# Operands of the dense products at staggered byte offsets in a hybrid decoder trunk

## The chip, the cores and the metric

One core of one Trainium2 chip runs the whole kernel. The metric is the device time of one execution in microseconds (us). Times of single products are given in nanoseconds (ns). TensorE's clock has two levels, 1.2 and 2.4 GHz; the profile gives the granted clock as a share of the higher one.

## What is computed

Two pre-RMSNorm residual layers over 512 tokens of width 1024, and a last RMSNorm. Layer 0 mixes tokens with 8 stick-breaking and 8 sparse-attention heads, layer 1 with 16 forgetting-attention heads, and each layer ends with a gated MLP whose one branch runs through a causal convolution of width 3:

```python
def conv_glu_ffn(h, w_in, conv_w, conv_b, w_out):          # w_in 1024 x 5632, w_out 2816 x 1024
    a, b = jnp.split(h @ w_in, 2, axis=-1)
    a = conv_general_dilated(a, taps, padding=[(2, 0)], ...) + conv_b
    return (jax.nn.silu(a) * b) @ w_out

for layer in range(DEPTH):
    h = rmsnorm(x, attn_norm[layer])
    x = x + (even_mixer if layer % 2 == 0 else odd_mixer)(h, ...)   # h @ w_in, attention, o @ w_out
    x = x + conv_glu_ffn(rmsnorm(x, ffn_norm[layer]), ...)
return rmsnorm(x, final_norm)
```

All of it is float32. What the change touches are the dense products: `h @ w_in` and `o @ w_out` of both mixers, and the two products of each MLP.

## The kernel before

Activations lie transposed, channels on the 128 partitions and 512 tokens along them. The normed input is held in 8 chunks of 128 channels, and each chunk twice, split into a high part `XH[k]` and the rest `XL[k]` (`xh`, `xl` in the profile), both in the reduced format fp32r. A weight block is split in the same way: `weights` loads it as `wraw`, ScalarE casts it to the high part `whi` (L193), VectorE subtracts to get `wlo` (L194). A dense product is then three products on TensorE for each chunk, accumulated in one PSUM bank (`unit`):

```python
for k in range(NK):
    mm(ps, h[:, k], XH[k], k == 0, False)        # whi[k] loaded as weights, xh[k] moves
    mm(ps, l[:, k], XH[k], False, False)         # wlo[k] loaded, xh[k] moves
    mm(ps, h[:, k], XL[k], False, k == NK - 1)   # whi[k] loaded, xl[k] moves
```

`mm(out, l, r, ...)` (L115) is one weight load of 128 columns (`l`) and one product in which 512 columns of `r` move through the array. A unit is 24 such products. `proj` does the same for the output products, with the 11 chunks `gh`, `gl` of half an MLP's inner activation, or the attention's `oh`, `ol` (in layer 0 for the NSA heads `o4` and `o6`), in the place of `xh`, `xl`. `vgroup` turns the operands round: slices of `XH[k]` are loaded as weights and 256 to 272 columns of `whi` or `wlo` move. `finish` is the last two columns of blocks of the second MLP, in pieces of 320 and 192 columns.

The program runs in stages: layer 0's input products, its attention with dense units laid between the heads' work (`Fill` hands them out), its output product, the first MLP, layer 1 in the same order, the second MLP. In an MLP, `fl` holds 22 units of the input product for each half (11 pairs of `a` and `b`, `wfi`), then 8 of `proj`. `use_a` and `use_b` scale what a unit gives by `rstd`, convolve, apply SiLU and write `gh` (ScalarE, L795) and `gl` (VectorE, L796). All tiles come from pools that place them one behind another in each partition, so the size of a tile decides where the next one begins.

Below, **place** is the first byte of an operand in its partition, as the built program has it. Before, with c the chunk:

| operand | first place | next chunk | place modulo 256 |
|---|---|---|---|
| `xh` / `xl` | 26656 / 43040 | +2048 | 32 |
| `whi` (two buffers), `wlo` (two) | 89120, 93472; 97824, 102176 | +512 | 32 |
| `gh` / `gl` (14 buffers each) | 127008 / 155680 | +2048 | 32 |
| layer 0 `o4` / `o6` | 127008 / 172448 | +2048 | 32 / 160 |
| layer 1 `oh4` to `oh6`, `ol4` to `ol6` / `oh7`, `ol7` | 203424, 217760 / 223968, 226016 | +2048 | 160 / 224 |

While one product runs, the weights of the next one are loaded. The **distance** of a product is the place of its own moving operand less the place of the weights that the next product takes, modulo 256. Counted over the built program: 4153 fp32r products of 512 columns are followed by another fp32r product; 3847 of them have distance 0, and the other 306 belong to `oh`, `ol` and `o6`.

Of the kernel before, what the change touches and what calls it, by code (L numbers as in the profile page):

```python
# [10 lines left out]
F32R = mybir.dt.float32r  # L11
BF = mybir.dt.bfloat16
# [5 lines left out]
P = 128  # L18
SEQ = 512
D = 1024  # L20
NK = D // P
# [83 lines left out]
def trunk(ctx, tc, A):  # L105
# [3 lines left out]
    cp = EP(tc.tile_pool(name="cp", bufs=1))  # L109
    xp = EP(tc.tile_pool(name="xp", bufs=1))  # L110
    wp = EP(tc.tile_pool(name="wp", bufs=2))
    pp = EP(tc.tile_pool(name="pp", bufs=2, space=PSUM))

    def mm(out, l, r, st, sp_):
        pe.matmul(out, l, r, start=st, stop=sp_)  # L115
# [7 lines left out]
    def table(last=None):  # L123

        if last is None:
            return act.preload_act_table_set("natural_log_exp_and_others").ins
        with tc.issue_after(last):
            return act.preload_act_table_set("natural_log_exp_and_others").ins
# [18 lines left out]

        return xp.tile(shape, dt, tag=f"x{n}", name=name)

    XH = [xp.tile([P, SEQ], F32R, name=f"xh{c}") for c in range(NK)]  # L150
    XL = [xp.tile([P, SEQ], F32R, name=f"xl{c}") for c in range(NK)]
    ng = cp.tile([P, 5, NK], F32, name="ng")
    rstd = cp.tile([P, SEQ], F32, name="rstd")
    rtok = cp.tile([P, NB], F32, name="rtok")
# [12 lines left out]

    def warm():

        z = cp.tile([P, SEQ], BF, name="zero")  # L170
        pool.memset(z, 0.0)
        ps = pp.tile([P, SEQ], F32, tag="t", bufs=1, name="t")
        for n in range(12):
            mm(ps, z[:, 0:P], z, n == 0, n == 11)


    def weights(src, shape, alloc=None, pieces=1):

        w = wp.tile(shape, F32, tag="wraw", bufs=2, name="wraw")
        if pieces > 1:  # L180
            h = wp.tile(shape, F32R, tag="whi", bufs=2, name="whi")
            l = wp.tile(shape, F32R, tag="wlo", bufs=2, name="wlo")
            n = shape[1] // pieces
            for c in range(0, shape[1], n):
                sp.dma_start(w[:, c:c + n], src[:, c:c + n])
            return h, l, w
        sp.dma_start(w, src)
        if alloc is not None:
            h, l = alloc(shape)
        else:  # L190
            h = wp.tile(shape, F32R, tag="whi", bufs=2, name="whi")
            l = wp.tile(shape, F32R, tag="wlo", bufs=2, name="wlo")
        act.copy(h, w)  # L193
        dve.tensor_sub(l, w, h.bitcast(F32))  # L194
        return h, l

    def unit(src, use, ps=None, hl=None):

        h, l = weights(src, [P, NK, P]) if hl is None else hl
        yield  # L200
        ps = pp.tile([P, SEQ], F32, tag="mm", bufs=2, name="mm") if ps is None else ps()
        for k in range(NK):
            mm(ps, h[:, k], XH[k], k == 0, False)
            mm(ps, l[:, k], XH[k], False, False)
            mm(ps, h[:, k], XL[k], False, k == NK - 1)
            if k == NK - 1:
                use(ps)
            yield

    def vgroup(srcs, n, use, allocs=(None, None)):  # L210

        ws = [weights(s, [P, NK // 2, n], a) for s, a in zip(srcs, allocs)]
        yield
        for tb in range(NB):
            t = slice(tb * P, tb * P + P)
            ps = pp.tile([P, SEQ], F32, tag="mm", bufs=2, name="mm")
            for k in range(NK):
                h, l = ws[k // 4]
                o = ps[:, 0:n]
                mm(o, XH[k][:, t], h[:, k % 4], k == 0, False)  # L220
                mm(o, XH[k][:, t], l[:, k % 4], False, False)
                mm(o, XL[k][:, t], h[:, k % 4], False, k == NK - 1)
                if k == NK - 1:
                    use(tb, ps)
                if k % 2 == 1:
                    yield
# [14 lines left out]
    def feed(c, layer):  # L241

        scale_x(c, layer)
        squares(c)

    def scale_x(c, layer):
        g = ng[:, layer, c:c + 1]
        act.activation(XH[c], X[c], AF.Copy, scale=g)  # L248
        dve.scalar_tensor_tensor(XL[c], X[c], g, XH[c].bitcast(F32), op0=ALU.mult, op1=ALU.subtract)  # L249

# [80 lines left out]
    def norm_stats(tok):  # L331
        st = s_banks()
        ps, ps2 = st[:, 0], st[:, 1]
        mm(ps, ones, ACC[0], True, True)
        inv_sqrt(rstd, ps, SEQ)
        if tok:
            for tb in range(NB):
                mm(ps2[:, tb:tb + 1], ACC[0][:, tb * P:tb * P + P], ones[:, 0:1], True, True)
            inv_sqrt(rtok, ps2[:, :NB], NB)
# [133 lines left out]
    def proj(m, srcs, oh, ol, use=None, ready=None):  # L473

        n = len(oh)
        ws = [(weights(src, [P, kn, P]), kn) for src, kn in srcs]
        yield
        while ready is not None and not ready():
            yield "wait"
        ps = pp.tile([P, SEQ], F32, tag="mm", bufs=2, name="mm")  # L480
        k = 0
        for (h, l), kn in ws:
            for kk in range(kn):
                mm(ps, h[:, kk], oh[k], k == 0, False)
                mm(ps, l[:, kk], oh[k], False, False)
                mm(ps, h[:, kk], ol[k], False, k == n - 1)
                k += 1
                if k == n:
                    dve.tensor_add(X[m], X[m], ps)  # L489
                    if use is not None:  # L490
                        use(m)
                yield


    def layer0():
        with ExitStack() as es:
# [85 lines left out]
            load_x(True)  # L582
            table()
            warm()
            for c in range(NK):
                if c % 2 == 0:
# [181 lines left out]
    def ffn(layer, nl, final):  # L768
        with ExitStack() as es:
            fp = es.enter_context(tc.tile_pool(name=f"fp{layer}", bufs=2))  # L770
            fl = Fill()
            for half in range(2):
                GH, GL = [], []

                def pair(c):
                    cw = conv[:, layer, c]
                    box = []

                    def use_a(ps):
                        a = fp.tile([P, SEQ], F32, tag="a", bufs=2, name="a")  # L780
                        t = fp.tile([P, SEQ], F32, tag="tt", bufs=2, name="tt")
                        box.append(t)
                        dve.tensor_mul(a, ps, rstd)  # L783
                        act.activation(t, a, AF.Identity, bias=cw[:, 3:4], scale=cw[:, 2:3])
                        dve.scalar_tensor_tensor(t[:, 2:], a[:, :SEQ - 2], cw[:, 0:1], t[:, 2:], op0=ALU.mult, op1=ALU.add)
                        dve.scalar_tensor_tensor(t[:, 1:], a[:, :SEQ - 1], cw[:, 1:2], t[:, 1:], op0=ALU.mult, op1=ALU.add)  # L786
                        silu.append(act.activation(t, t, AF.Silu).ins)  # L787

                    def use_b(ps):
                        b = fp.tile([P, SEQ], F32, tag="b", bufs=2, name="b")  # L790
                        dve.tensor_mul(b, ps, rstd)  # L791
                        dve.tensor_mul(b, b, box[0])
                        gh = fp.tile([P, SEQ], F32R, tag="gh", bufs=14, name="gh")
                        gl = fp.tile([P, SEQ], F32R, tag="gl", bufs=14, name="gl")
                        act.copy(gh, b)  # L795
                        dve.tensor_sub(gl, b, gh.bitcast(F32))  # L796
                        GH.append(gh)
                        GL.append(gl)
                    return unit(A["wfi"][layer, 2 * c], use_a), unit(A["wfi"][layer, 2 * c + 1], use_b)

                for c in range(11 * half, 11 * half + 11):
                    fl.add(*pair(c))
                if not half:
                    fl.step(NK - 1)
                    norm_stats(False)
                fl.all()
                if half:
                    table(silu[-1])
                src = lambda m: [(A["wfo6"][layer, m, half], 6), (A["wfo5"][layer, m, half], 5)]
                use = (final if final else lambda m: feed(m, nl)) if half else None  # L810
                if half and final:
                    fl.add(*[proj(m, src(m), GH, GL, use) for m in range(NK - 2)])
                    fl.all()
                    finish(fp, src, GH, GL)
                    return
                fl.add(*[proj(m, src(m), GH, GL, use) for m in range(NK)])
                fl.all()

    ffn(0, 2, None)


# [120 lines left out]
    def last(m):  # L942

        squares(m)
        act.activation(X[m], X[m], AF.Copy, scale=ng[:, 4, m:m + 1])
    ffn(1, 4, last)


# [94 lines left out]
```

## Time and profile before

| what | value |
|---|---|
| median of 2 timed runs | 1290.58 us (1289.38 to 1291.78) |
| the profiled execution | 1291.93 us, span 1290.1 us from its first to its last instruction |
| TensorE busy | 1271.2 us, 99% of the span |
| VectorE / ScalarE / GpSimd busy | 693.7 / 555.7 / 147.9 us |
| granted clock | 0.997 on average |
| HBM | 119.28 MB read, 94 GB/s over the span with the writes |

The busy time of a product in this profile is modelled: products are pipelined, a row of 0.39 us overlaps the next one. What a product costs in a row of products is the step from its start to the next start, so the timelines below are read by their starts.

### The profile page before, as it was taken

Reading aid. Unit: us, or ns where it says so; the run is one execution under the profiler, and the core shown is the slowest. Engines: PE = TensorE matmul, PEld = TensorE weight load, DVE = VectorE, ACT = ScalarE, POOL = GpSimd, SP = SyncE. Lnnn points to the kernel's source line nnn. Section 1 sums busy time; section 2 is a strip of 40 time slices with the busy share of each in tenths; the row PEclk is TensorE's granted clock in tenths of the full one; section 3 lists DMA queues with packets and bytes.
Section 4 is the critical chain, followed back from the end, with each engine's and each line's share of the span. In section 5 each row is a group of like instructions: output and inputs, shape, how many; then the busy total and the mean of one; then the engine's idle time right before and its main releaser. Section 6 shows DMA issues by size and latency. Waiting matters only on the chain.

```text
span 1290.1 us, 16521 instructions
## 1 busy us (share of the span) xinstructions
PE 1271.2 (99%) x6338; PEld 1002.1 (78%) x6338; DVE 693.7 (54%) x1142; ACT 555.7 (43%) x948; POOL 147.9 (11%) x206
## 2 busy tenths in 40 slices
PE   8999999999999999999999999999999999999997
PEld 5876856567888888888888877866788888888886
DVE  7468665538655434565443443344755543556534
ACT  6556465645433223334342554444533322333442
POOL 0000042223000000000111433321200000000010
PEclk9999999999999999999999999999999999999999
DMA  6315201003333233232344453411333223333232
GB/s 224 95 59 147 87 21 42 19 26 123 98 99 94 78 106 107 92 98 89 94 127 141 145 151 92 120 51 51 122 98 98 88 90 100 108 94 94 88 99 90
DMA packets 50639, 124.00 MB, mean 96 GB/s; under 512 B 6320, under 2 KB 15792, under 8 KB 50560
## 3 DMA queue, kind: packets, MB, share of 16 engines
q1 hardware_dynamic: 49040, 121.35, 31.0%
q10 hardware_dynamic: 1520, 1.59, 0.4%
q8 instruction: 50, 0.82, 0.3%
q14 instruction: 29, 0.24, 0.1%
HBM read 119.28 MB, written 2.13 MB: 94 GB/s over the span
## 4 chain that ended last, share of the span: by engine, by line
PE 93%; DVE 3%; ACT 2%; issue 1%; DMA 1%; SPq 0%; DVEq 0%; ACTq 0%
PE mm L115 80%; PE s L115 6%; PE o L115 4%; PE t L425 3%; DVE e L462 1%; DVE wlo L194 0%; ACT whi L193 0%; DMA x<-x 0%; ACT xh L248 0%; DMA wraw<-wu 0%; DVE lt L457 0%; DVE acc L239 0%; ACT lt L454 0%; DVE e L463 0%; DVE e L401 0%
## 5 line engine op out<-in xcount | busy, mean ns | idle before, releaser
L115 PE MATMUL mm<-xh,whi 128*128 128x512 f32 x936 | 372.2, 398 | 0.9 <-ACT xh L248 0.6
L115 PE MATMUL mm<-xh,wlo 128*128 128x512 f32 x936 | 365.1, 390 | 1.6 <-DVE wlo L194 1.6
L115 PE MATMUL mm<-xl,whi 128*128 128x512 f32 x936 | 365.5, 391 | 0.1
L193 ACT CAST whi<-wraw 128x1024 fp32r<-128x1024 f32 (+2 forms) x219 | 200.0, 914 | 383.5 <-PE mm L115 362.7
L194 DVE TENSOR_TENSOR wlo<-wraw,whi 128x1024 fp32r<-128x1024 f32 (+2 forms) x219 | 236.4, 1079 | 137.4 <-ACT whi L193 134.7
L115 PEld LDWEIGHTS mm<-xh,whi 128*128 128x128 f32 x936 | 175.8, 188 | 44.8 <-issue 8.8
L115 PEld LDWEIGHTS mm<-xl,whi 128*128 128x128 f32 x936 | 175.8, 188 | 40.0 <-DVE xl L249 1.8
L115 PEld LDWEIGHTS mm<-xh,wlo 128*128 128x128 f32 x936 | 176.1, 188 | 37.0 <-DVE wlo L194 2.2
L115 PE MATMUL mm<-gh,whi 128*128 128x512 f32 (+2 forms) x352 | 135.0, 383 | 0.0
L115 PE MATMUL mm<-gl,whi 128*128 128x512 f32 (+2 forms) x352 | 134.8, 383 | 0.0
L115 PE MATMUL mm<-gh,wlo 128*128 128x512 f32 (+2 forms) x352 | 134.8, 383 | 0.0
L416 POOL TENSOR_SCALAR e<-e,dn 128x512 f32<-128x512 f32 (+3 forms) x128 | 78.1, 629 | 176.9 <-DVE dn L410 83.9
L403 ACT ACTIVATE e<-e,nm 128x512 f32<-128x512 f32 (+3 forms) x128 | 70.4, 551 | 50.2 <-DVE nm L401 50.2
L426 ACT COPY ph<-t 128x512 f32<-128x512 f32 x100 | 58.1, 581 | 69.6 <-PE t L425 69.4
L783 DVE TENSOR_TENSOR a<-mm,rstd 128x512 f32<-128x512 f32 x44 | 30.4, 691 | 92.1 <-PE mm L115 91.9
L237 POOL COPY acc<-sq 128x512 f32<-128x512 f32 x4 | 2.8, 706 | 651.4 <-ACT sq L234 651.4
L489 DVE TENSOR_TENSOR x<-x,mm 128x512 f32<-128x512 f32 x62 | 42.6, 686 | 64.2 <-PE mm L115 63.9
L115 PEld LDWEIGHTS mm<-gh,wlo 128*128 128x128 f32 x352 | 66.1, 188 | 13.0
L115 PEld LDWEIGHTS mm<-gl,whi 128*128 128x128 f32 x352 | 66.1, 188 | 12.8
L115 PEld LDWEIGHTS mm<-gh,whi 128*128 128x128 f32 x352 | 66.1, 188 | 12.8
L791 DVE TENSOR_TENSOR b<-mm,rstd 128x512 f32<-128x512 f32 x44 | 30.4, 692 | 72.4 <-PE mm L115 72.3
L787 ACT ACTIVATE tt<-tt 128x512 f32<-128x512 f32 x44 | 27.8, 632 | 86.8 <-DVE tt L786 86.8
(167 smaller groups left out, 1644.3 us busy)
## 6 DMA issues: line engine op xcount, KB each, us to landing
wraw<-wfi SPq DMA_DIRECT2D x88, 512.0 KB
wraw<-wu SPq DMA_DIRECT2D x31, 512.0 KB
wraw<-wfo SPq DMA_DIRECT2D x32, 384.0 KB
wraw<-wfo SPq DMA_DIRECT2D x32, 320.0 KB
wraw<-wo SPq DMA_DIRECT2D x32, 256.0 KB
cb<-cd SPq DMA_DIRECT2D x8, 512.0 KB
x<-x SPq DMA_DIRECT2D x14, 256.0 KB
wraw<-wv SPq DMA_DIRECT2D x6, 528.0 KB
```

The source lines that it names most:

```text
L115: pe.matmul(out, l, r, start=st, stop=sp_)
L193: act.copy(h, w)
L194: dve.tensor_sub(l, w, h.bitcast(F32))
L403: act.activation(ei, ei, AF.Exp, bias=nm, scale=-1.0, accum_out=dn)
L416: pool.tensor_scalar(ei, ei, self.dn[:, hd, i:i + 1], 1.0, op0=ALU.mult, op1=ALU.mult)
L425: pe.transpose(ps[:, o:o + P], self.e[:, hd, EOFF[i] + j * P:EOFF[i] + j * P + P], ident)
L426: act.copy(self.ph[:, 512 * n:512 * n + 512], ps)
L462: dve.tensor_tensor_scan(ei[:, ::-1], li[:, ::-1], li[:, ::-1], 0.0, op0=ALU.add, op1=ALU.bypass)
L489: dve.tensor_add(X[m], X[m], ps)
L783: dve.tensor_mul(a, ps, rstd)
L787: silu.append(act.activation(t, t, AF.Silu).ins)
L791: dve.tensor_mul(b, ps, rstd)
```

## The change

No instruction is added, taken away or moved: on each engine the two built programs list the same instructions in the same order, and they differ in where tiles lie in SBUF, and in one wait.

- `XH` and `XL` tiles get 8 more elements, so each chunk lies 2080 bytes behind the last instead of 2048. Chunk c begins at 25632 + 2080c (`xl`: 42272 + 2080c): modulo 256 that is 32 + 32c.
- `parts` allocates `whi` and `wlo` with 64 elements more than they need and puts the block `shift` elements in. In each half of an MLP the 22 units of the input product take the 22 pairs of `steps` (0 to 48 elements, 0 to 192 bytes, for `whi` and `wlo` apart); all other blocks take (0, 0). The buffers begin at 88608, 93216, 97824 and 102432, 32 modulo 256.
- `gh` and `gl` get 64 more elements, and chunk j of a half lies 4j bytes (`gh`) or 16j bytes (`gl`) into its place; the places themselves are 32 modulo 256 as before.
- `zero`, the operand of the warm-up products, moves from a pool of its own into the `sq` buffers. ScalarE's first square (L234) takes the same buffer and now waits for the warm-up products and the memset of `zero`.
- All tiles behind these move by 512 bytes, their places modulo 256 unchanged: `q`, `k`, `e`, `ph`, `oh`, `ol`, `o4`, `o6` and the rest.

By the built program, of the 3803 products of 512 columns in which `xh`, `xl`, `gh` or `gl` moves, 3801 had distance 0 before. Now 396 have it; 1857 have a distance from 96 to 224, and 1550 another one (4 to 92, or 228 to 252). The distance of a product in the input product changes with each chunk, that is after each third product.

```diff
-    XH = [xp.tile([P, SEQ], F32R, name=f"xh{c}") for c in range(NK)]
-    XL = [xp.tile([P, SEQ], F32R, name=f"xl{c}") for c in range(NK)]
+    XH = [xp.tile([P, SEQ + 8], F32R, name=f"xh{c}")[:, 0:SEQ] for c in range(NK)]
+    XL = [xp.tile([P, SEQ + 8], F32R, name=f"xl{c}")[:, 0:SEQ] for c in range(NK)]
...
-        z = cp.tile([P, SEQ], BF, name="zero")
+        z = wp.tile([P, SEQ], BF, tag="sq", bufs=2, name="zero")
...
+    SHIFT = [(0, 0)]
+
+    def parts(shape, shift):
+
+        n = shape[1] * shape[2]
+        out = []
+        for tag, o in zip(("whi", "wlo"), shift):
+            t = wp.tile([P, n + 64], F32R, tag=tag, bufs=2, name=tag)
+            out.append(t[:, o:o + n].rearrange("p (k m) -> p k m", m=shape[2]))
+        return out
...
+        shift = SHIFT.pop(0) if len(SHIFT) > 1 else SHIFT[0]
...
-            h = wp.tile(shape, F32R, tag="whi", bufs=2, name="whi")
-            l = wp.tile(shape, F32R, tag="wlo", bufs=2, name="wlo")
+            h, l = parts(shape, shift)
...
+                steps = ((0, 0), (0, 32), (32, 0), (0, 16), (16, 0), (0, 48), (48, 0), (0, 8), (8, 0), (0, 1), (1, 0),
+                         (0, 2), (2, 0), (0, 4), (4, 0), (4, 4), (8, 8), (16, 16), (24, 0), (0, 24), (40, 0), (0, 40))
+                SHIFT[:] = list(steps) + [(0, 0)]
...
-                        gh = fp.tile([P, SEQ], F32R, tag="gh", bufs=14, name="gh")
-                        gl = fp.tile([P, SEQ], F32R, tag="gl", bufs=14, name="gl")
+                        j = c % 11
+                        gh = fp.tile([P, SEQ + 64], F32R, tag="gh", bufs=14, name="gh")[:, j:j + SEQ]
+                        gl = fp.tile([P, SEQ + 64], F32R, tag="gl", bufs=14, name="gl")[:, 4 * j:4 * j + SEQ]
```

## Rows read from the trace of the kernel before

**Rows 1.** The page of the profile: busy time of each engine (its share of the span, its instructions), and the chain of work that ended last, by engine and by line.

```profile
PE 1271.2 (99%) x6338; PEld 1002.1 (78%) x6338; DVE 693.7 (54%) x1142; ACT 555.7 (43%) x948; POOL 147.9 (11%) x206
...
PE 93%; DVE 3%; ACT 2%; issue 1%; DMA 1%; SPq 0%; DVEq 0%; ACTq 0%
PE mm L115 80%; PE s L115 6%; PE o L115 4%; PE t L425 3%; DVE e L462 1%; DVE wlo L194 0%; ACT whi L193 0%; DMA x<-x 0%; ACT xh L248 0%; DMA wraw<-wu 0%; DVE lt L457 0%; DVE acc L239 0%; ACT lt L454 0%; DVE e L463 0%; DVE e L401 0%
```

**Rows 2.** Groups of TensorE's instructions over the whole span, shapes kept apart: line, engine, operation, result and operands (the moving one first, the one that is loaded as weights second), shape, count, then busy us, mean ns of one, and idle us of the engine just before them.

```profile
L115 PE MATMUL mm<-xh,whi 128*128 128x512 f32 x936 | 372.2, 398 | 0.9 <-ACT xh L248 0.6
L115 PE MATMUL mm<-xl,whi 128*128 128x512 f32 x936 | 365.5, 391 | 0.1
L115 PE MATMUL mm<-xh,wlo 128*128 128x512 f32 x936 | 365.1, 390 | 1.6 <-DVE wlo L194 1.6
L115 PE MATMUL mm<-gh,whi 128*128 128x512 f32 x330 | 128.4, 389 | 0.0
L115 PE MATMUL mm<-gl,whi 128*128 128x512 f32 x330 | 128.4, 389 | 0.0
L115 PE MATMUL mm<-gh,wlo 128*128 128x512 f32 x330 | 128.4, 389 | 0.0
```

**Rows 3.** TensorE's timeline over one unit of the first FFN's input product (24 products; the last row is the first product of the next unit): start in us, us of one, engine, line, operation, result and operands.

```profile
500.24 0.39 PE L115 MATMUL mm<-xh,whi 128*128 128x512 f32 x1
500.46 0.39 PE L115 MATMUL mm<-xh,wlo 128*128 128x512 f32 x1
500.69 0.39 PE L115 MATMUL mm<-xl,whi 128*128 128x512 f32 x1
...
505.68 0.39 PE L115 MATMUL mm<-xh,whi 128*128 128x512 f32 x1
```

**Rows 4.** Two stretches of 300 us, one in each FFN: start and end, length, TensorE's busy us and its products begun, granted clock as a share of full speed, DMA share and GB/s.

```profile
340.00:640.00 300.00, 300.00 (x1325) 1.00 0.31 96
960.00:1260.00 300.00, 300.00 (x1325) 1.00 0.32 96
```

**Rows 5.** TensorE's timeline at the first 32 products of `finish`, 320 columns wide: the first, and the last that is not merged with another kind.

```profile
1261.42 0.30 PE L115 MATMUL mm<-gh,fh 128*128 128x320 f32 x1
...
1266.11 0.31 PE L115 MATMUL mm<-gl,fh 128*128 128x320 f32 x1
```

**Rows 6.** TensorE's timeline over two units (24 products) of the output product of layer 1: the first, two in the middle, and the first of the next unit.

```profile
904.87 0.39 PE L115 MATMUL mm<-oh,whi 128*128 128x512 f32 x1
...
906.25 0.40 PE L115 MATMUL mm<-oh,whi 128*128 128x512 f32 x1
906.49 0.40 PE L115 MATMUL mm<-oh,wlo 128*128 128x512 f32 x1
...
910.44 0.39 PE L115 MATMUL mm<-oh,whi 128*128 128x512 f32 x1
```

**Rows 7.** TensorE's timeline where the output product of layer 0 ends (its last product starts at 308.29) and the first unit of the first FFN begins: its first, fourth and seventh product.

```profile
308.52 0.39 PE L115 MATMUL mm<-xh,whi 128*128 128x512 f32 x1
...
309.22 0.39 PE L115 MATMUL mm<-xh,whi 128*128 128x512 f32 x1
...
309.90 0.39 PE L115 MATMUL mm<-xh,whi 128*128 128x512 f32 x1
```

**Rows 8.** TensorE's timeline over 24 products of layer 0's second value group, where slices of `xh` and `xl` are loaded as weights and 264 columns of `vhi`, `vlo`, `whi` and `wlo` move: the first of three of the groups of three, the one behind them, and the first product of the next block of rows.

```profile
61.32 0.28 PE L115 MATMUL mm<-vhi,xh 128*128 128x264 f32 x1
...
61.68 0.28 PE L115 MATMUL mm<-vhi,xh 128*128 128x264 f32 x1
...
62.05 0.28 PE L115 MATMUL mm<-vhi,xh 128*128 128x264 f32 x1
...
62.40 0.28 PE L115 MATMUL mm<-vhi,xh 128*128 128x264 f32 x1
...
64.21 0.28 PE L115 MATMUL mm<-vhi,xh 128*128 128x264 f32 x1
```

**Rows 9.** The stretch of the first FFN: start and end, length, busy us and instructions of PE, PEld, DVE, ACT and POOL, granted clock, DMA share and GB/s.

```profile
308.50:667.00 358.50, 358.37 (x1579) 296.09 (x1578) 190.25 (x237) 128.44 (x162) 11.42 (x9) 1.00 0.32 98
```

**Rows 10.** Groups of VectorE's and ScalarE's instructions from 340 to 640 us that write the operands of the products: line, engine, operation, out<-in, shape, count, busy us, mean ns of one, idle us before them and what ended it.

```profile
L194 DVE TENSOR_TENSOR wlo<-wraw,whi 128x1024 fp32r<-128x1024 f32 (+2 forms) x63 | 68.4, 1086 | 43.2 <-ACT whi L193 42.1
L796 DVE TENSOR_TENSOR gl<-b,gh 128x512 fp32r<-128x512 f32 x20 | 13.7, 685 | 1.4 <-ACT gh L795 1.4
L193 ACT CAST whi<-wraw 128x1024 fp32r<-128x1024 f32 (+2 forms) x63 | 59.5, 944 | 145.2 <-PE mm L115 145.1
L795 ACT CAST gh<-b 128x512 fp32r<-128x512 f32 x20 | 12.5, 624 | 11.4 <-DVE b L792 11.4
```

**Rows 11.** The start: TensorE's warm-up products and ScalarE's first square, from the timelines of the two engines.

```profile
1.35 5.00 PE L115 MATMUL t<-zero 128*128 128x512 bf16 x12 [1.35 <-POOL zero L171]
...
12.26 0.61 ACT L234 ACTIVATE sq<-x 128x512 f32<-128x512 f32 x1
```

More of the change, by code (lines that the diff above doesn't have):

```diff
@@ L190, in weights @@
         else:
-            h = wp.tile(shape, F32R, tag="whi", bufs=2, name="whi")
-            l = wp.tile(shape, F32R, tag="wlo", bufs=2, name="wlo")
+            h, l = parts(shape, shift)
         act.copy(h, w)
```

## The prediction, made before the changed kernel was run

> **What bounds the kernel now.** I read the page first: TensorE is busy 99% of the span, 93% of the chain that ended last is on it, and 80% is the one line L115 with result `mm`, the dense products [rows 1]. Nothing else comes near, so what counts is what one dense product costs. The groups of TensorE's instructions say how many there are: 3 x 936 with `xh` or `xl` moving and 3 x 330 with `gh` or `gl`, 3798 in all, with idle time of 2.6 us in front of the first three groups together and none in front of the others [rows 2]. Their "mean ns" (389 to 398) can't be summed, since one product overlaps the next; the cost is the step from start to start.
>
> Step by step, then, on the timeline. A unit of 24 products in the MLP takes 505.68 - 500.24 = 5.44 us, 226.7 ns a product [rows 3]. Two stretches of 300 us hold 1325 products each, 226.4 ns with the ones at the edges counted whole, TensorE busy all the time at full granted clock, the level of 2.4 GHz [rows 4]. There is no jitter to win back there: nothing waits, and every step is the same. What of the 226.7 ns is columns? In `finish`, 320 columns take (1266.11 - 1261.42) / 32 = 146.6 ns [rows 5]. 192 columns less save 80.1 ns, 0.417 ns a column. So 512 columns are 213.5 ns, and **13.2 ns a product** don't depend on the width. These 13.2 ns are all that a change of places can act on: 3798 times, 50 us.
>
> **Do they depend on places?** The trace has three stretches in which distances are not 0.
> - Layer 1's output product, all distances 128 or 192: 24 products in 910.44 - 904.87 = 5.57 us, 232.1 ns each; single steps differ (906.25 to 906.49 is 240) [rows 6]. That is 5.4 ns a product above the MLP, with the same operations at the same width.
> - From such products into the MLP's, at distance 0: the first three steps take 309.22 - 308.52 = 0.70 us (233 ns each), the next three 0.68 (227) [rows 7]. So even at distance 0 the short step has to be reached, and it took three products.
> - The value group, 264 columns: 24 products in 64.21 - 61.32 = 2.89 us, 120.4 ns each. 264 columns are 110.1 ns by the price above, so 10.3 ns are left, less than 13.2, although the distances there run through all multiples of 32. Its groups of three differ: at distances 160, 32, 160 the three take 0.37 us (13.2 ns over the columns), at 192, 64, 192 0.35 us (6.6 ns over them) [rows 8].
>
> Places do matter, by a few ns a product, to both sides.
>
> **The change, part by part.** No instruction is added or moved, so its whole price is in the steps.
> 1. *Chunks 32 bytes apart, shifted weights, shifted `gh` and `gl`.* 3407 products leave distance 0 (1857 to distances from 96 to 224, 1550 to others), and nearly all the rest no longer stand in a row of equal distance. For a product of 512 columns at distance 128 or 192 there is a row: +5.4 ns. I take it for the 1857: 10.0 us. For the other 1550 no row has a product of this width at their distances. The bounds are +5.4 ns (as in rows 6, and as at the entry in rows 7) and -2.9 ns (10.3 against 13.2, as in rows 8). I take half of the loss, +2.7 ns, since rows 7 show that a new distance starts on a long step, and here a new one comes after each third product: 4.2 us. The 396 at distance 0 I leave. Sum **+14.2 us**. Bounds for all 3407: +5.4 ns is +18.4 us, -2.9 ns is -9.9 us, and the best group of three (-6.6 ns) would be -22.5 us.
> 2. *Writes of shifted operands.* ScalarE's casts and VectorE's subtractions write at odd multiples of 4 bytes. The trace has no such write. In the first MLP VectorE is busy 190 of 358 us and ScalarE 128 [rows 9]. If the groups that write `wlo` and `gl` cost twice as much, VectorE would have 82.1 us more in 300 [rows 10], a share of 53 + 27 = 80%; ScalarE 128 / 358 + 72 / 300, 60%. TensorE covers both, so 0. Without that cover it would be those microseconds.
> 3. *`zero` in the `sq` buffers.* The first square starts at 12.26, the warm-up products end at 6.35 [rows 11]. The new wait is over 5.9 us before it is reached; behind it nothing moves. 0.
> 4. *Value groups.* Their distances ran through all multiples of 32 and do so again in another order. 640 products by the difference of the groups of three (6.6 ns) would be 4 us either way; I take 0.
>
> Against the profiled execution: span 1290.1 + 14.2 = 1304.3, an execution of 1306.1. That execution (1291.93) lies 1.35 us above the median of the runs shown, so on that scale 1290.6 + 14.2 = 1304.8; I say 1304.
>
> **A rule that says otherwise.** The row: equal products take 226.7 or 232.1 ns, and the places of their operands are what differs [rows 3, 6]. The Trainium skill, "TensorE: Matmul & The Clock Gate", section "Step-by-step: what each phase is for", holds that TensorE reads the moving operand and the next weights through two independent ports, so that loading weights takes no read bandwidth from the running product. By that rule the sum of part 1 is 0; by the rows it is +14.2 us. The trace does not agree with the rule as far as it goes, and I follow the trace.
>
> **The rivals.**
> - *Nothing changes.* Layer 1's 232.1 ns might come from something else than distance: its operands lie elsewhere in SBUF, and other work runs beside it. Then the steps stay at 226.7 and the time is 1290.6. Against it: in rows 7 the same operands at the same place go from 233 to 227 ns within three products, so it is a state that two streams of reads fall into, and the groups of three in rows 8 differ by place alone. Some distances may also keep the short step, with a mean loss of 1 or 2 ns: 1294 to 1297.
> - *It gets faster.* If products of 512 columns at mixed distances behave as the value group does, each saves 2.9 ns: 1290.6 - 9.9 = 1280.7; with the price of the best three everywhere, 1268.1. It decides if the mean step in the MLP's input product falls below 226.7. For it: the value group is the one place where all distances occur. Against it: at a width of 512 no stretch shows less than 226.7, and distance 192, good in the value group, is in the slow rows of layer 1.
> - *It gets slower by more than 2%.* That needs 25.8 us, 7.6 ns on each of the 3407, a mean step of 234.3. Single steps of 240 exist [rows 6], a mean over a unit as high as that does not. It would take distances that no row shows, such as those of the weights and of `gh` that are no multiple of 16 bytes. With 240 in all of them: 1290.6 + 3407 x 13.3 = 1335.9.
> - *VectorE becomes the bound* in the MLP by slow shifted writes: worked out in part 2, needs more than a doubling. Very unlikely, and then a matter of some tens of us.
>
> **How the numbers follow.** A mean loss of 2.2 to 5.4 ns (1298 to 1309): 0.45, and its middle is the forecast. About nothing (1287 to 1298): 0.23. Faster, 1265 to 1287: 0.13. A loss beyond 5.4 ns but below 2% (1309 to 1316): 0.05. Slower by more than 2%: 0.10. Faster by more than 2% (below 1264.8; it needs the step at 219 ns, less than the best three): 0.04. The range from **1282 to 1316** leaves out about 0.08 below and 0.10 above, and holds both signs; the likeliest case alone is 1298 to 1309. About 2% is what a measurement of this kernel can tell from no change: faster 0.04, within it 0.86, slower 0.10.
>
> **What would show it.** In the changed profile the count of products is the same and so is the granted clock. Right: in the MLP a unit of 24 takes 5.50 to 5.57 us in place of 5.44, more where its chunks lie at distances from 96 to 224; two stretches of 300 us hold some 20 products fewer; layer 1's output product stays at 232 ns. Wrong in sign: units of 5.37 us, or groups of three at 220 ns. Wrong in place: gaps in front of `mm` with VectorE or ScalarE as the releaser, or a busy time of L194 and L193 that has grown by tens of us and shows up on the chain. The forecast fails if the short step holds at any distance, or if the distances without a row are much worse than 128 and 192.

## The result, and the profile after

| | before | after |
|---|---|---|
| median | 1290.58 us (1289.38 to 1291.78) | 1307.91 us (1307.88 to 1307.95) |
| span of the profiled execution | 1290.1 us | 1306.1 us |

The ratio is 1.0134, 95% interval 1.0091 to 1.0178: 17.3 us longer, and within 2%.

The page of the profile after: busy time of each engine, and the chain of work that ended last, by engine and by line.

```profile
PE 1288.0 (99%) x6338; PEld 1001.4 (77%) x6338; DVE 693.9 (53%) x1142; ACT 555.4 (43%) x948; POOL 146.7 (11%) x206
...
PE 95%; DVE 2%; ACT 2%; DMA 1%; issue 1%; SPq 0%; DVEq 0%
PE mm L115 81%; PE s L115 7%; PE o L115 4%; PE t L436 3%; DMA x<-x 0%; DVE e L473 0%; ACT xh L259 0%; ACT whi L204 0%; DMA wc<-wcv 0%; DVE acc L250 0%; DVE lt L468 0%; DVE wlo L205 0%; ACT lt L465 0%; DVE e L474 0%; DVE e L412 0%
```

TensorE is still the only bound, busy 99%; its busy time has grown by 16.8 us (1271.2 in [rows 1]), while VectorE and ScalarE are as before (693.7, 555.7). Groups of TensorE's instructions, shapes kept apart (busy us, mean ns of one, idle us in front):

```profile
L115 PE MATMUL mm<-xh,whi 128*128 128x512 f32 x936 | 376.1, 402 | 1.2 <-ACT xh L259 1.2
L115 PE MATMUL mm<-xl,whi 128*128 128x512 f32 x936 | 369.7, 395 | 0.1
L115 PE MATMUL mm<-xh,wlo 128*128 128x512 f32 x936 | 369.1, 394 | 1.4 <-DVE wlo L205 1.4
L115 PE MATMUL mm<-gh,whi 128*128 128x512 f32 x330 | 129.6, 393 | 0.0
```

Same counts as in [rows 2], no new idle time in front of them (2.7 us in all, 2.6 before), and each mean about 4 ns higher. So the time is in the products themselves. The two stretches of 300 us (TensorE's busy us, its products begun, granted clock, DMA share, GB/s):

```profile
340.00:640.00 300.00, 300.00 (x1294) 1.00 0.30 94
960.00:1260.00 300.00, 300.00 (x1295) 1.00 0.30 93
```

1294 and 1295 products instead of 1325 [rows 4], at the same full clock: 300 / 1294 = 231.8 ns each against 226.4, **5.4 ns more**. The MLPs hold 88 units of 24 and 990 output products, 3102 of 512 columns; 3102 x 5.4 = 16.8 us, which covers the 16.0 us of the span. By the first and last products on TensorE's timeline the first MLP goes from 360.35 to 368.67 us and the second, up to `finish`, from 350.23 to 358.24; what lies before the first MLP is 1.0 us shorter, layer 1's mixer 0.6 us longer, and the rest is the same. The 1.0 us says nothing of the change: that stretch took 308.5 us in this trace of the kernel before and 306.6 in the run with two pads (below), where nothing in it differs.

One unit of the first FFN on TensorE's timeline, with `whi` 64 and `wlo` 0 bytes into their places, all distances multiples of 32 (the first product, two in the middle, the first of the next unit):

```profile
514.65 0.40 PE L115 MATMUL mm<-xh,whi 128*128 128x512 f32 x1
...
516.76 0.40 PE L115 MATMUL mm<-xh,whi 128*128 128x512 f32 x1
517.00 0.39 PE L115 MATMUL mm<-xh,wlo 128*128 128x512 f32 x1
...
520.25 0.39 PE L115 MATMUL mm<-xh,whi 128*128 128x512 f32 x1
```

24 products take 5.60 us, 233 ns each; single steps go up to 0.24 us. In [rows 3] they took 5.44 and every step was alike. All the units of the MLP's input product that run without a gap lie between 5537 and 5606 ns, whatever their distances. Layer 1's output product, whose places the change leaves alone, over 24 products:

```profile
909.32 0.39 PE L115 MATMUL mm<-oh,whi 128*128 128x512 f32 x1
...
914.89 0.39 PE L115 MATMUL mm<-oh,whi 128*128 128x512 f32 x1
```

5.57 us, as in [rows 6]. Last, three groups that write the shifted operands, VectorE's and ScalarE's between 340 and 640 us (count, busy us, mean ns of one, idle us in front):

```profile
L205 DVE TENSOR_TENSOR wlo<-wraw,whi 128x1024 fp32r<-128x1024 f32 (+2 forms) x61 | 66.6, 1092 | 41.3 <-ACT whi L204 40.4
L204 ACT CAST whi<-wraw 128x1024 fp32r<-128x1024 f32 (+2 forms) x61 | 57.7, 945 | 147.2 <-PE mm L115 147.2
L811 ACT CAST gh<-b 128x512 fp32r<-128x512 f32 x20 | 12.4, 622 | 11.5 <-DVE b L807 11.5
```

1092, 945 and 622 ns against 1086, 944 and 624 in [rows 10]. The first two means mix block sizes, and few of their blocks stand at odd multiples of 4 bytes; `gh` does in every second chunk (`gl`, shifted by multiples of 16 bytes, never does). In the run below that shifts the weights by every multiple of 4 bytes, VectorE's `wlo` of 128x1024 takes 1223 ns against 1222 before, and ScalarE's `whi` 1050 against 1056. So writing to odd multiples of 4 bytes costs nothing that these rows show.

### The profile page after: what moved, and what is told of

The parts are those of the page before. It is cut to its first block, busy times and chain, and to the rows that moved or that the text cites. A ratio compares the mean times of both kernels' runs of the same rounds, so it can differ in the third digit from the quotient of the medians.

```text
span 1306.1 us, 16522 instructions
## 1 busy us (share of the span) xinstructions
PE 1288.0 (99%) x6338; PEld 1001.4 (77%) x6338; DVE 693.9 (53%) x1142; ACT 555.4 (43%) x948; POOL 146.7 (11%) x206
## 4 chain that ended last, share of the span: by engine, by line
PE 95%; DVE 2%; ACT 2%; DMA 1%; issue 1%; SPq 0%; DVEq 0%
PE mm L115 81%; PE s L115 7%; PE o L115 4%; PE t L436 3%; DMA x<-x 0%; DVE e L473 0%; ACT xh L259 0%; ACT whi L204 0%; DMA wc<-wcv 0%; DVE acc L250 0%; DVE lt L468 0%; DVE wlo L205 0%; ACT lt L465 0%; DVE e L474 0%; DVE e L412 0%
## 5 line engine op out<-in xcount | busy, mean ns | idle before, releaser
L115 PE MATMUL mm<-xh,whi 128*128 128x512 f32 x936 | 376.1, 402 | 1.2 <-ACT xh L259 1.2
L115 PE MATMUL mm<-xh,wlo 128*128 128x512 f32 x936 | 369.1, 394 | 1.4 <-DVE wlo L205 1.4
L115 PE MATMUL mm<-xl,whi 128*128 128x512 f32 x936 | 369.7, 395 | 0.1
L798 DVE TENSOR_TENSOR a<-mm,rstd 128x512 f32<-128x512 f32 x44 | 30.4, 691 | 97.7 <-PE mm L115 97.5
L806 DVE TENSOR_TENSOR b<-mm,rstd 128x512 f32<-128x512 f32 x44 | 30.4, 691 | 78.3 <-PE mm L115 78.3
```

## The experiments

The words of the theories: **D**, the loss is a matter of a product's own distance; **P**, of the place itself; **C**, of the distance changing from product to product. Later **S**: the short step needs distance 0 *and* each kind of operand at the same place (modulo 256) from product to product; **P2**: it needs the place 32.

### The parts of the change by themselves

Chunks 2080 bytes apart and nothing else shifted (`gh` and `gl` in their wide places, all 32 modulo 256):

```diff
-                SHIFT[:] = list(steps) + [(0, 0)]
-    gh = ...[:, j:j + SEQ]      gl = ...[:, 4 * j:4 * j + SEQ]
+    gh = ...[:, 0:SEQ]          gl = ...[:, 0:SEQ]
```

> One part of the change alone: chunks of xh and xl 2080 bytes apart; weight blocks unshifted; gh and gl in places of 2304 bytes but unshifted, so distance 0. Three theories. D (distance): the short step of 226.7 ns is reached only in a row of products at distance 0, all else runs near 232. P (place): the step depends on where an operand itself begins, not on the difference of two. C (change): a change of the distance from product to product costs, its value does not. All three expect the MLP's input product at about 232 ns a step (its unit of 24 at 5.56 us) and the MLP's output product, whose places are wider but whose distance is 0, back at 226.7 (33 products in 7.48 us). Time: about 12 us over before, 1301 to 1304. If the wider places of gh and gl mattered by themselves, the output product would not be back.

1304.63 us against 1289.73 for the kernel before in the same session, ratio 1.0114 (1.0099 to 1.0129): +14.9 us. 24 products of the output product, and a unit of the input product (TensorE's timeline: the first product of each, and the first behind it):

```profile
440.37 0.39 PE L115 MATMUL mm<-gh,whi 128*128 128x512 f32 x1
...
445.81 0.39 PE L115 MATMUL mm<-gh,whi 128*128 128x512 f32 x1
...
526.87 0.40 PE L115 MATMUL mm<-xh,whi 128*128 128x512 f32 x1
...
532.45 0.40 PE L115 MATMUL mm<-xh,whi 128*128 128x512 f32 x1
```

5.44 us where nothing is staggered, 5.58 where the chunks are. Every chunk then has its own distance, 0 among them; the unit repeats with one pattern of steps between 226 and 238 ns, and the three products at distance 0 take 231 ns on average, hardly less than the rest. 80 of the 88 units take 5580 ns to within 1 ns, whatever VectorE, ScalarE and the DMA do beside them, which speaks against a collision with their work. The 2304 bytes from one `gh` to the next do no harm: they are a multiple of 256.

Only `gh` and `gl` shifted, by 4j and 16j bytes:

```diff
-                SHIFT[:] = list(steps) + [(0, 0)]
-    XH = [xp.tile([P, SEQ + 8], ...)[:, 0:SEQ] ...]     (XL alike)
+    XH = [xp.tile([P, SEQ], ...)[:, 0:SEQ] ...]
```

> The other part alone: gh shifted by 4j bytes and gl by 16j, chunks of xh and xl 2048 apart and weight blocks unshifted. All three theories: input product at 226.7 ns a step, output product near 231.5; 990 products of about 4.9 ns more are 4.8 us, so about 1295.5. This and the chunks alone should add up to the change, with nothing left for the shifted weights, if a product that has lost the short step can lose it only once.

1295.57 us, ratio 1.0047 (1.003 to 1.0063): +5.8 us. The output product on TensorE's timeline:

```profile
440.10 0.39 PE L115 MATMUL mm<-gh,whi 128*128 128x512 f32 x1
...
445.66 0.39 PE L115 MATMUL mm<-gh,whi 128*128 128x512 f32 x1
```

5.56 us for 24, 231.7 ns each, while the input units are back at 5.44. 990 x 5 ns is 5.0 us, about what the time shows. The expectation that this and the chunks alone add up to the change can't be read from the times: 14.9 + 5.8 = 20.7 us against 17.3, with intervals of about 2 us on the parts and 6 on the whole. By the steps it holds: 88 units x 0.14 us is 12.3 us with the chunks, 5.0 us here, together 17.3, against 16.8 in the MLPs of the change. The shifts of the weights added nothing on top.

Only the weight parts' shifts in the units of the input product:

```diff
-    XH = [xp.tile([P, SEQ + 8], ...)[:, 0:SEQ] ...]     (XL alike)
-    ...[:, j:j + SEQ]      ...[:, 4 * j:4 * j + SEQ]
+    XH = [xp.tile([P, SEQ], ...)[:, 0:SEQ] ...]
+    ...[:, 0:SEQ]          ...[:, 0:SEQ]
```

> Only the third part of the change: the shifts of the weight parts, with chunks 2048 bytes apart and gh and gl unshifted. By counts 1150 products of the MLP's input product then stand at another distance than 0 and 880 of the same units still at 0. If each product pays by its own distance: 1150 x 5.6 ns = 6.4 us, units about 5518 ns, time 1297. Theory S (a product at another place also costs its neighbours the short step): all 84 shifted units at 5540 to 5600 ns, 11.7 us, time 1302. With the other two parts, 14.9 and 5.8 us by themselves, the sum is over the 17.3 us of the whole in both cases, since the chunks and the shifts act on the same products.

1299.15 us against 1289.41, ratio 1.0079 (1.0063 to 1.0095): +9.7 us, between the two expectations. First products of units on TensorE's timeline: with (`whi`, `wlo`) shifted by (0, 0), then by (0, 128) bytes, then the one behind; and of the unit with (16, 0), `whi` 16 bytes on and `wlo` in place, and the one behind it:

```profile
489.36 0.39 PE L115 MATMUL mm<-xh,whi 128*128 128x512 f32 x1
...
494.80 0.40 PE L115 MATMUL mm<-xh,whi 128*128 128x512 f32 x1
...
500.35 0.40 PE L115 MATMUL mm<-xh,whi 128*128 128x512 f32 x1
...
567.13 0.39 PE L115 MATMUL mm<-xh,whi 128*128 128x512 f32 x1
...
572.58 0.39 PE L115 MATMUL mm<-xh,whi 128*128 128x512 f32 x1
```

5.44 us, 5.55 us, and 5.45 us in the last. Most shifted units take 5527 to 5610 ns, as S expects; but with (16, 0) the steps are back at 227 ns from the third on, and the next unit, both parts 16 bytes on, goes on like that (5448 ns), and the one with (96, 0) takes 5513. So another place for the weights is not always a loss. The times of the three parts sum to 30.4 us where the whole is 17.3: chunks and weight shifts act on the same products, and a product loses its short step only once.

### Is it the distance?

Distance the same throughout a unit: chunks 2048 bytes apart, `gh` and `gl` unshifted, and both weight parts of a unit shifted by the same amount, 0 to 224 bytes in steps of 32:

```diff
+                steps = ((0, 0), (0, 0), (8, 8), (8, 8), (8, 8), (16, 16), ..., (56, 56), (56, 56))
```

> Chunks 2048 apart, gh and gl unshifted, and in each unit of the MLP's input product whi and wlo shifted by the same amount, two or three units in a row with 0, 32, 64, 96, 128, 160, 192 and 224 bytes. So the distance is the same for all 24 products of a unit and runs through all multiples of 32 from unit to unit. D expects 226.7 in the units at distance 0 and about 232 at all the others: 1280 products x 5.3 ns in each half of the kernel's two MLPs scaled to 1920 in all, 10 us, about 1301. C expects 226.7 everywhere but for three or so products behind each change: 1291 to 1292. P expects long steps wherever the weights are shifted, as D. A distance with a step under 226.7, which none of the three asks for, would be of use.

1301.56 us (one execution). Units at distance 0 and at distance 64 (weights shifted by 192 bytes) on TensorE's timeline, first product and first of the next:

```profile
490.62 0.39 PE L115 MATMUL mm<-xh,whi 128*128 128x512 f32 x1
...
496.06 0.39 PE L115 MATMUL mm<-xh,whi 128*128 128x512 f32 x1
...
585.40 0.39 PE L115 MATMUL mm<-xh,whi 128*128 128x512 f32 x1
...
590.89 0.39 PE L115 MATMUL mm<-xh,whi 128*128 128x512 f32 x1
```

5.44 and 5.49 us. All other distances settle between 5571 and 5626 ns: a distance that stays the same is not enough, so C falls. Each unit falls into a short pattern that repeats (232, 235, 232, 235 at a shift of 32 bytes; 226, 229, 232 at distance 64).

The opposite: distance 0 everywhere, with places that move on. `xh` and the weights' chunks are staggered together by 32 bytes a chunk (the weights' chunks 544 bytes apart), `xl` 32 bytes further on than `xh`, so that it too meets its next weights at distance 0:

```diff
+        m = shape[2] + (8 if shape[1:] == [NK, P] else 0)
+            out.append(t.rearrange("p (k m) -> p k m", m=m)[:, :, 0:shape[2]])
```

> Moving chunks and weight chunks staggered together: chunk c of xh 32c bytes on, chunk k of whi and wlo 32k bytes on (544 bytes from one to the next), xl 32 bytes further on than xh, so that each product finds its next weights at distance 0 although the places of both run through all multiples of 32 as in the change. gh and gl unshifted. D and C expect 226.7 ns a step everywhere, 1290 to 1292. P expects the input product as in the change, near 232, about 1302.

1303.42 us, ratio 1.0106 (1.0091 to 1.0121). A unit, on the timeline:

```profile
512.93 0.39 PE L115 MATMUL mm<-xh,whi 128*128 128x512 f32 x1
...
518.51 0.39 PE L115 MATMUL mm<-xh,whi 128*128 128x512 f32 x1
```

5.58 us, steps 231, 227, 236, 234, 236, 232 in turn. With this D falls, the theory that the prediction was built on: the products of the units are at distance 0 here, and they are long.

### Which places

The input product's weights shifted by every multiple of 4 bytes in turn; the output product's three kinds of operand shifted together by 32, 64, 128 and 20 bytes in the four halves:

```diff
+                n = 22 * (2 * layer + half)
+                at = (8, 16, 32, 5)[2 * layer + half]
+                SHIFT[:] = [(o % 64, o % 64) for o in range(n, n + 22)] + [(at, at)]
...
+    gh = ...[:, at:at + SEQ]     gl = ...[:, at:at + SEQ]
```

> The chunks are 2048 bytes apart as before. In the MLP's input product the two weight parts of each unit are shifted together, by every multiple of 4 bytes in turn, so the distance is the same within a unit and all 64 of them occur. In the output product gh, gl and their weights are shifted together by 32, 64, 128 and 20 bytes in the four halves, so the distance is 0 there at four other places. Theory S (the short step comes where the distance is 0 and each kind of operand stands at the same place from product to product): the output product keeps 226.7 ns in all four halves. Theory P2 (it needs the place 32 itself): the output product rises to about 232 ns in all four halves. For the input product both expect 226.7 ns at distance 0, 229 at distance 64 and about 232 elsewhere; a step below 226.7 at any distance would be new to both. Time 1300 to 1302 under S, 1302 to 1306 under P2.

1302.56 us (one execution). On TensorE's timeline, in order: 24 output products with all operands shifted by 32 bytes; the units of the input product whose weights stand at 180 and at 188 modulo 256, `xh` and `xl` at 32; 24 output products with all operands shifted by 20 bytes. Again the first product of each and the first behind:

```profile
439.69 0.39 PE L115 MATMUL mm<-gh,whi 128*128 128x512 f32 x1
...
445.13 0.39 PE L115 MATMUL mm<-gh,whi 128*128 128x512 f32 x1
...
573.41 0.39 PE L115 MATMUL mm<-xh,whi 128*128 128x512 f32 x1
...
579.01 0.39 PE L115 MATMUL mm<-xh,whi 128*128 128x512 f32 x1
...
584.57 0.39 PE L115 MATMUL mm<-xh,whi 128*128 128x512 f32 x1
...
590.02 0.39 PE L115 MATMUL mm<-xh,whi 128*128 128x512 f32 x1
...
1234.61 0.39 PE L115 MATMUL mm<-gh,whi 128*128 128x512 f32 x1
...
1240.25 0.39 PE L115 MATMUL mm<-gh,whi 128*128 128x512 f32 x1
```

5.44 us; 5.60 and 5.45; 5.64. At 32, 64 and 128 bytes the output product keeps 226.7 ns, so P2 falls and S holds there. P in its plain form falls too: products with weights at place 64 are long beside `xh` at 32 in the run with one distance a unit, and short here beside `gh` and `gl` at 64. At 20 bytes the output product takes 235.0, although the distance is 0 and all stand at one place. In the scan, unexpected by all theories, six other places of the weights (4, 28, 152, 164, 176 and 188) also settle at 227 ns, so distance 0 is not needed. None of the 64 settles below it; the worst, 196, takes 5703 ns with single steps of 257. And the places do not fix the step alone: with both parts at 48 a unit takes 5598 ns here, behind a unit of long steps, and 5448 in the run with the weight shifts alone, behind one that had settled at 227. So what ran before counts too.

How fine the places may be: the output product's operands all shifted by 4, 8, 16 and 96 bytes.

```diff
-                at = (8, 16, 32, 5)[2 * layer + half]
+                at = (1, 2, 4, 24)[2 * layer + half]
```

> Input product as before. In the output product gh, gl and their weights are shifted together by 4, 8, 16 and 96 bytes in the four halves, so distance 0 and one place for all, as at 20 bytes (235.0 ns) and at 32, 64 and 128 bytes (226.7). Theory S with whole 32 bytes as its grain: 226.7 at 96 bytes alone, 232 to 235 at 4, 8 and 16; time about 1290.6 + 790 x 7 ns = 1296. With whole 16 bytes as the grain: 226.7 at 16 too, 1294. If only odd places such as 20 are bad for another reason, 226.7 at 8 and 16 as well, 1292.

1296.9 us (one execution). 24 output products at 4, 16 and 96 bytes on the timeline:

```profile
439.56 0.40 PE L115 MATMUL mm<-gh,whi 128*128 128x512 f32 x1
...
445.26 0.40 PE L115 MATMUL mm<-gh,whi 128*128 128x512 f32 x1
...
1050.01 0.39 PE L115 MATMUL mm<-gh,whi 128*128 128x512 f32 x1
...
1055.53 0.39 PE L115 MATMUL mm<-gh,whi 128*128 128x512 f32 x1
...
1229.67 0.39 PE L115 MATMUL mm<-gh,whi 128*128 128x512 f32 x1
...
1235.11 0.39 PE L115 MATMUL mm<-gh,whi 128*128 128x512 f32 x1
```

5.70, 5.52 and 5.44 us; over whole blocks of 33 products 237.8, 230.0 and 226.7 ns a product (8 bytes: 231.1). Of the eight shifts that were tried, those by whole 32 bytes keep the short step, as the first case of the expectation has it, and the others do not; that case had put 4, 8 and 16 bytes at 232 to 235 ns, which none of the three took.

### A bad place mended

The kernel before with two pads, so that layer 1's `oh` and `ol` all stand at 32:

```diff
+            c1.tile([P, 32], F32, name="gap")
             OH = [c1.tile([P, SEQ], F32R, name=f"oh{c}") for c in range(NK - 1)]
...
-            bf = c1.tile([P, 16], F32, name="bf")
+            bf = c1.tile([P, 64], F32, name="bf")[:, 0:16]
```

> The kernel before with two pads, by which oh and ol of layer 1 lie at the same place modulo 256 as the weights, so that its output product (192 products that took 232.1 ns each) stands at distance 0. If places alone made those products slow: 24 of them take 5.44 us in place of 5.57, and the time falls by 192 x 5.4 ns = 1.0 us to 1289.5, too little to tell by the interval but plain in the trace. If something else made them slow (the operands' far place in SBUF, the work beside them): they stay at 5.57 us.

Layer 1's output product on the timeline, two products 24 apart:

```profile
904.58 0.39 PE L115 MATMUL mm<-oh,whi 128*128 128x512 f32 x1
...
910.02 0.39 PE L115 MATMUL mm<-oh,whi 128*128 128x512 f32 x1
```

24 products in 5.44 us, where [rows 6] had 5.57: the place was the reason. Not all 192 products get there: by their steps they take 0.6 us less together (46.7 against 47.3), where 1.0 was expected. The time is 1289.23 against 1289.41 us, ratio 0.9997 (0.9988 to 1.0006), and 0.6 us is less than the interval can tell, so no version here is measurably faster than the kernel before.

### What the 13.2 ns are

Half of the weights' columns for one product in three, places as before:

```diff
-            mm(ps, l[:, k], XH[k], False, False)
-            mm(ps, h[:, k], XL[k], False, k == NK - 1)
+            mm(ps[0:64], h[:, k, 0:64], XL[k], False, False)
+            mm(ps, l[:, k], XH[k], False, k == NK - 1)
```

> Places as before. Each unit's product with xl takes only the first 64 columns of its weights and gives only the first 64 rows (the low part of the activations is left out for the other 64). Its 512 moving columns stay. Theory W (the 13.2 ns over the columns are the time that reading the next weights costs): the step before each such product falls by 6 to 7 ns, a unit from 5440 to about 5387 ns, the time by 6 us to 1284. Theory F (a fixed cost between two products): units stay at 5440 ns, time 1290.

1298.05 us (one execution): slower, which neither theory had. The weight loads of the changed product and of one beside it (busy us, mean ns of one, idle us in front):

```profile
L115 PEld LDWEIGHTS mm<-xl,whi 128*64 128x64 f32 x936 | 126.0, 135 | 39.3 <-DVE xl L249 2.1 <-issue 0.5
L115 PEld LDWEIGHTS mm<-xh,wlo 128*128 128x128 f32 x936 | 175.8, 188 | 90.4 <-DVE wlo L194 1.9 <-issue 1.0
```

A unit on the timeline, its first product and the first of the next:

```profile
507.01 0.39 PE L115 MATMUL mm<-xh,whi 128*128 128x512 f32 x1
...
512.52 0.40 PE L115 MATMUL mm<-xh,whi 128*128 128x512 f32 x1
```

The load is 53 ns shorter (135 against 188), and the 24 products take 5.51 us instead of 5.44; the steps run between 224 and 236 ns and never settle at 227. The edit also puts the products of a chunk in another order, so that was run with whole weights:

> The order of the three products of a chunk as in the run with half loads (h with xh, h with xl, l with xh), with whole weights and the places of before. If loading 64 columns in place of 128 was what broke the regular step there: units are back at 5440 ns and the time at 1290. If the order did it (all three then alternate whi, whi, wlo): units stay near 5515 ns, time 1298. Theory S by itself expects 5440, since distance and places are those of before.

A unit of it:

```profile
504.83 0.39 PE L115 MATMUL mm<-xh,whi 128*128 128x512 f32 x1
...
510.27 0.39 PE L115 MATMUL mm<-xh,whi 128*128 128x512 f32 x1
```

5.44 us, and 1290.7 us in all against 1290.02 for the kernel before (one execution each): the order is harmless. So it was the half loads that broke the short step, or the products on half the rows that go with them; the edit changes both. Less work made the steps longer. W and F both fail, since neither has a step that grows when a load gets shorter. What the 13.2 ns consist of is not shown.

## Why the prediction came out as it did

The forecast was 1304 us; 1307.9 came out, inside the range and inside its likeliest case (1298 to 1309).

- **What bounds the kernel.** Right: the loss is in TensorE's steps, no gap appeared in front of any product.
- **Part 1, the 1857 products at distances from 96 to 224.** Taken at +5.4 ns from [rows 6]. The 1422 of them in the MLPs (counted from the places under "The change") came out at 232.7 ns a step, +6.0, and the run with two pads shows that the row was read rightly: layer 1's 232 ns came from places.
- **Part 1, the 1550 at other distances.** This is the term that was mis-sized: half of the loss, +2.7 ns, 4.2 us. The 1374 of them in the MLPs took 231.6 ns, +4.9 where +2.7 was taken; at that price the term is 7.6 us. The bound of -2.9 ns from the value group [rows 8] was no guide: no unit of 512 columns settled below 226.7 in any run.
- **Part 1, the 396 left at distance 0.** Taken at nothing; the 306 in the MLPs took 231.4 ns, +4.8, so 396 x 4.8 = 1.9 us. The step that failed is the idea behind the count, that a product's own distance prices it: the three classes differ by little over 1 ns, and with distance 0 everywhere and places that move on, units take 5.58 us.
- **Part 1, outside the MLPs.** Some 700 of the 3803 products stand there. The forecast took them as leaving the short step, but before the change their steps averaged 229.7 ns (steps over 260 ns, which hold a wait, left out), so they had less to lose: 232.4 after, about 1.9 us.
- **How near the sum is.** The terms inside the MLPs were too small by 5 us and the one outside about 1 us too large, so that +14.2 stands against some 18.7 us by the steps. The 17.3 us between the medians is smaller, but the two runs of the kernel before lie 2.4 us apart, and 14 later ones have a median of 1289.41 us; the true loss may be nearer 18.5. That the forecast lay so close to the result is in part luck.
- **The signs named.** The count and the clock are unchanged and layer 1's output product stays at 5.57 us, as forecast. Units take 5.54 to 5.61 us where 5.50 to 5.57 was said, and the two stretches hold 31 and 30 products fewer where some 20 was said.
- **Parts 2 to 4.** Right at 0: the writes' durations above, no new wait on the chain, and over all 640 products of the value groups the steps grew by 0.1 us together.
- **The rivals.** *Nothing changes* is excluded by the interval. *Faster* needed a step below 226.7, and none holds. *Slower by more than 2%* needed a mean step of 234.3, which whole stretches show only with all operands 4 or 20 bytes off, or with single places of the weights in the scan. *VectorE becomes the bound* failed, with its durations unchanged.
- **The rule that says otherwise.** Units with chunks in place and only the weights shifted go from 5.44 to as much as 5.61 us, with no more bytes read. So where the weights lie reaches the step of the products. The Trainium skill, "TensorE: Matmul & The Clock Gate", section "Step-by-step: what each phase is for", holds that loading the next weights takes no read bandwidth from the running product. The sum of 0 that the prediction drew from this did not come. But no run here shows that bandwidth is what was lost: the weight loads' own rows keep 188 ns before and after, and half the weights made the steps longer.

That places alone make the loss is shown; why they do stays open. The runs say which of the tried places give the short step, not what in the chip repeats with 256 and 32 bytes, nor why six other places of the weights give it too, or why the same places settle in two ways.

## What to carry to other kernels

When TensorE is busy 99% with equal products, read the steps from start to start, not the busy shares: here a row of steps that agree to 1 ns was the short state, and steps that scatter by a few ns marked operands that lie badly. For fp32r products of 512 columns with a new weight load each, keep every moving operand and every weight block at the same place modulo 256 and on whole 32 bytes (32, 64, 96, 128 and 160 modulo 256 were tried), and let tiles that come between have sizes that keep it so; staggered operands cost 2.4% of the step here and no run gave anything back. A pad in one pool can shift all tiles behind it, so look at the places after each change of a tile's size.

## What the runs showed of the hardware that was not expected

- The step of a dense product is not the price of its columns plus a share of its weight load. With equal places on whole 32 bytes it is 226.7 ns; otherwise it mostly runs in patterns that repeat and average 229 to 238 ns, and with one weight load in three 53 ns shorter it was 3 ns longer.
- The short step has to be reached: in the run with shifted output operands (by 32 bytes) eight long steps came first (234, 229, 231, 231, 236, 228, 233, 230, then 227).
- Distance 0 with everything 4 bytes off a multiple of 32 costs 11 ns a product; 16 bytes off costs 3.3.
